# RWKV time mixing on one core: a weight's load between the halves of unit 0, coefficients worked out on rows, and one unit's transposes one step later

## The chip, the cores and the metric

The kernel runs on one core of a Trainium2 chip. The metric is device time in microseconds (us) of one execution. Five engines work beside each other, each in its own order: PE (matmul; its weight loads are shown apart as PEld), DVE (vector), ACT (scalar), POOL (GpSimd) and SP (which here only issues DMAs). They wait for each other through semaphores. ACT, POOL and SP issue DMAs; a queue's descriptors are worked off by 16 DMA engines.

## The reference

For x of 16 batches, 2048 tokens and 256 channels:

```python
x_prev[:, 1:, :] = x[:, :-1, :]
xv = x * time_mix_v + x_prev * (1 - time_mix_v)
xr = x * time_mix_r + x_prev * (1 - time_mix_r)
v = xv.reshape(-1, d_model) @ value_weight
r = xr.reshape(-1, d_model) @ receptance_weight
r_sigmoid = 1.0 / (1.0 + np.exp(-r))
out = (r_sigmoid * v).reshape(-1, d_model) @ output_weight
```

The key path (xk, k) does not enter the output, and the kernel does not compute it.

## The kernel before, in words

A **unit** is 512 tokens, so there are 64 units, four to a batch. PE needs the channels on the partitions, so x is transposed first: for the first ten batches on PE (`transposes`, L260, into `ps_t`, copied to the transposed tiles `xt_...` by ACT), for the last ones by DMA. In the transposed tile the previous token is the same data one slot to the left, so no second copy of x is made.

Mixing is folded into the weights. With s = time_mix and p = 1 - s, x·s + x_prev·p = s·(x + c·x_prev) with c = 1/s - 1. The weights are scaled by s once (`w_bf`), and per unit DVE (with POOL and ACT helping) scales the previous tokens by c (`scale`, L351) and adds the tokens (`add`, L374) into `mix`. Only R of unit 0 is made without a mix (`project_unmixed`, L398): four matmuls for each half of the output channels, two with `w_prev` (the weight times p) on the previous tokens and two with `w_bf`.

For each unit, in the order in which the loop over g (L646) writes it, PE does R (`psum_r`, L384), transposes of a later unit (`advance`, L659), V (`psum_v`, L384) and the output product O of the unit before (`psum_o`, L416). ACT applies the sigmoid (L658), copies transposes (L289) and outputs (L471). DVE multiplies the sigmoid with V (`z_sb`, L697). The order on each engine is that of the program; nothing is rescheduled. `psum_r`, `psum_v` and `psum_o` have one buffer each, `ps_t` has two.

How far the transposes run ahead is set by the table `START_T` (L73): behind R of unit g they go up to unit `START_T[g]`, and the loads that `LOADS` (L79) ties to a unit are issued on POOL when `advance` gets to it. With unit 5, batch 1's second unit, goes the load of batch 3 (`(1, 1): (3,)`).

**The head.** SP loads units 0 and 1 of x as float32 in halves of two of their four 128-token columns (`load_halves`, half 1 ahead of half 0, into a tile of the `o_sb` pool), with the first weight (receptance) behind unit 0 and the value weight behind unit 1. ACT loads the four rows of time_mix_r and time_mix_v (`tm_rows`). POOL waits until the first weight has landed, and then issues casting loads (float32 to bfloat16): units 2 and 3, the output weight, batch 1 by units, and later whole batches. PE warms up on constants (`warm_up`, L201), transposes half 1, the four rows (L236), half 0 in two parts (L300), and goes on to R of unit 0, the transposes of unit 1, the second half of R, V of unit 0. `coefficients` (L234) copies the transposed rows from PSUM and makes s, p and c on 128 partitions by 4 columns.

Of the kernel before, what the change touches and what calls it, by code (L numbers as in the profile page):

```python
# [8 lines left out]
FP32 = mybir.dt.float32  # L9
BF16 = mybir.dt.bfloat16  # L10
ALU = mybir.AluOpType
# [4 lines left out]
def kernel(  # L16
# [25 lines left out]
    nc = tc.nc  # L42

    B, S, D = x.shape
    P = 128
    KO = D // P
# [8 lines left out]
    H = UJ // 2  # L55
# [14 lines left out]
    PAD = 16  # L70
    SPARE = 9 * UB // 2
    NX, NO = 4, 7
    START_T = [1, 3, 5, 6, 7, 9, 11, 12]  # L73
    AHEAD = 6
    PAIRS = 10
    WARM = 25
# [14 lines left out]
    consts = ctx.enter_context(tc.tile_pool(name="consts", bufs=1))  # L91
# [20 lines left out]
    loads = {}  # L112
# [7 lines left out]
    ident_f = consts.tile([P, P], FP32)  # L120
# [26 lines left out]
    def load(b):  # L147
        if b < STAGED:
            x_bf[b] = xpool.tile([P, J, D], BF16, name="x_bf")
        if b < BYUNIT:  # L150
            for e in range(UB):
                nc.gpsimd.dma_start(  # L152
                    out=x_bf[b][:, e * UJ : (e + 1) * UJ, :], in_=unit_rows(x, b, e)[:, 0]
                )
            return
        if b in HALVED:
            return [
                nc.gpsimd.dma_start(out=x_bf[b][:, j : j + J // 2], in_=rows(b)[:, j : j + J // 2])
                for j in (0, J // 2)
            ]  # L160
        run = 8192 if b < LONG else 16384
        return nc.gpsimd.dma_start(out=x_bf[b], in_=rows(b), max_dma_last_dim=run)  # L162

    x_unit = opool.tile([P, 2, UJ, D], FP32, name="o_sb")
    tm_rows = consts.tile([2 * KO, P], FP32)
    w_f32 = consts.tile([P, 2, KO, D], FP32)
    for m, tm in enumerate([time_mix_r, time_mix_v]):
        nc.scalar.dma_start(
            out=tm_rows[m * KO : (m + 1) * KO, :], in_=tm.rearrange("(ko p) -> ko p", p=P)
        )  # L170

    def load_halves(e):
        for h in (1, 0):
            nc.sync.dma_start(  # L174
                out=x_unit[:, e, h * H : (h + 1) * H],
                in_=unit_rows(x, 0, e)[:, 0, h * H : (h + 1) * H, :],
            )

    load_halves(0)
    first_weight = nc.sync.dma_start(  # L180
        out=w_f32[:, 0], in_=receptance_weight.rearrange("(ko p) n -> p ko n", p=P)
    )
    load_halves(1)
    nc.sync.dma_start(out=w_f32[:, 1], in_=value_weight.rearrange("(ko p) n -> p ko n", p=P))
    sig0 = consts.tile([P, 1], BF16)
    nc.scalar.activation(out=sig0, in_=zeros[:, 0:1], func=ACT.Sigmoid)
# [1 line left out]
    w_prev = consts.tile([P, KO, D], BF16)  # L188
    wo_bf = consts.tile([P, KO, D], BF16)
    x_first = xpool.tile([P, 2, UJ, D], BF16, name="x_bf")  # L190
    for e in (2, 3):
        op = nc.gpsimd.dma_start(out=x_first[:, e - 2], in_=unit_rows(x, 0, e)[:, 0])  # L192
        if e == 2:
            tc.add_manual_dep(op.ins, first_weight.ins.name, SYNC, reason="behind the weight")
    nc.gpsimd.dma_start(out=wo_bf, in_=output_weight.rearrange("(ko p) n -> p ko n", p=P))  # L195
    load(1)

    ones = nc.const_aps.tensor_like(1.0, zeros)
    wide = nc.const_aps.tensor_like(1.0, wo_bf.rearrange("p k d -> p (k d)"))
# [10 lines left out]
    def new_xt(b):  # L210
        if b >= BYUNIT:
            for group in GROUPS:
                if b != group[0]:
                    continue
                if b >= STAGED:
                    t = xtpool.tile([P, KO, len(group) * (PAD + S)], BF16, name="xt_both")
                    for k in range(len(group)):
                        xt[b + k] = t[:, :, k * (PAD + S) + PAD - 1 : (k + 1) * (PAD + S)]
                    xt_both[b] = t
                    return  # L220
                xt_both[b] = xtpool.tile([P, J + 1, KO, len(group), P], BF16, name="xt_both")
                for k in range(len(group)):
                    xt[b + k] = xt_both[b][:, :, :, k]
                    nc.gpsimd.memset(xt[b + k][:, 0, :, 0:1], 0.0)
            return
        xt[b] = consts.tile([P, UB * (UJ + 1), KO, P], BF16, name=f"xt_first{b}")
        (nc.vector if b == 0 else nc.gpsimd).memset(xt[b][:, 0, :, 0:1], 0.0)

    new_xt(0)
    tms = consts.tile([P, 2, KO], FP32)  # L230
    c_sb = consts.tile([P, 2, KO], FP32)
    tm_prev = consts.tile([P, 2, KO], FP32)

    def coefficients():  # L234
        ps = ps_o_pool.tile([P, 2, KO], FP32, name="psum_o")
        nc.tensor.transpose(  # L236
            out=ps.rearrange("p m k -> p (m k)"), in_=tm_rows, identity=ident_f[: 2 * KO, : 2 * KO]
        )
        tm = consts.tile([P, 2, KO], FP32)
        nc.vector.tensor_copy(out=tm, in_=ps)  # L240
        nc.vector.tensor_scalar(
            out=tms, in0=tm, scalar1=0.0, scalar2=1e-30, op0=ALU.is_equal, op1=ALU.mult
        )
        nc.vector.tensor_tensor(out=tms, in0=tms, in1=tm, op=ALU.add)
        nc.vector.tensor_scalar(
            out=tm_prev, in0=tm, scalar1=-1.0, scalar2=1.0, op0=ALU.mult, op1=ALU.add
        )
        nc.vector.reciprocal(c_sb, tms)
        nc.vector.tensor_scalar(out=c_sb, in0=c_sb, scalar1=-1.0, scalar2=None, op0=ALU.add)

    def by_dma(b, after):

# [42 lines left out]
    def first_transposes():  # L295
        def part(lo, n, pool, name):
            ps = pool.tile([P, n, KO, P], FP32, name=name)
            for jj in range(n):
                for ko in range(KO):
                    nc.tensor.transpose(  # L300
                        out=ps[:, jj, ko],
                        in_=x_unit[:, 0, lo + jj, ko * P : (ko + 1) * P],
                        identity=ident_f,
                    )
            nc.scalar.copy(out=xt[0][:, 1 + lo : 1 + lo + n], in_=ps)
            return ps

        ps = part(H, H, ps_r_pool, "psum_r")
        nc.scalar.copy(out=xt[0][:, 0, :, 1:P], in_=ps[:, H - 1, :, 0 : P - 1])
        coefficients()  # L310
        part(0, 1, ps_v_pool, "psum_v")
        part(1, 1, ps_o_pool, "psum_o")

    def slots(piece, off=0):

        b, _, lo, hi = piece
        j = lo // P + (lo // TU if b < BYUNIT else 0) + off
        return slice(j, j + (hi - lo) // P)
# [32 lines left out]
    def scale(piece, kos=(0, 1)):  # L351
        b, m, _, _ = piece
        for ko in kos:
            nc.vector.tensor_scalar(  # L354
                out=mixed(piece, ko),
                in0=tokens(piece, 0, ko),
                scalar1=c_sb[:, m, ko : ko + 1],
                scalar2=None,
                op0=ALU.mult,
            )  # L360
# [205 lines left out]
    def advance(limit):  # L566
        nonlocal tnext
        while tnext <= min(limit, NU - 1):
# [4 lines left out]
                transposes(tnext)  # L573
            tnext += 1

    first_transposes()
    for ko in range(KO):
        nc.vector.tensor_scalar(
            out=w_prev[:, ko, :],
            in0=w_f32[:, 0, ko, :],  # L580
            scalar1=tm_prev[:, 0, ko : ko + 1],
            scalar2=None,
            op0=ALU.mult,
        )
    nc.vector.tensor_scalar(
        out=w_bf[:, 0, 0, :], in0=w_f32[:, 0, 0, :], scalar1=tms[:, 0, 0:1], scalar2=None, op0=ALU.mult
    )
    nc.scalar.activation(
        out=w_bf[:, 0, 1, :], in_=w_f32[:, 0, 1, :], func=ACT.Copy, scale=tms[:, 0, 1:2]
    )  # L590
    scale(pieces(0)[1])
    add(pieces(0)[1])
    for ko in range(KO):
        nc.vector.tensor_scalar(
            out=w_bf[:, 1, ko, :],
            in0=w_f32[:, 1, ko, :],
            scalar1=tms[:, 1, ko : ko + 1],
            scalar2=None,
            op0=ALU.mult,
# [11 lines left out]
    first = {}  # L611
# [34 lines left out]
    for g in range(NU - 1):  # L646
# [48 lines left out]
        n = TU // 2 if g == NU - 2 else TU  # L695
        for c in range(0, TU, n):
            nc.vector.tensor_tensor(  # L697
                out=z_sb[:, :, c : c + n],
                in0=s_sb[:, :, c : c + n],
                in1=ps_v[:, :, c : c + n],  # L700
                op=ALU.mult,
# [47 lines left out]
```

## Time and profile before

| | us |
|---|---|
| median of three runs | 199.56 |
| lowest and highest run | 198.65, 200.79 |
| span of the profiled execution | 197.1 |
| PE busy in it | 191.5 |
| DVE, ACT, POOL busy | 183.1, 177.1, 86.3 |

For the profiled execution the page gives its span, from the first instruction to the last, and no other time; what lies around the span is in the runs' times alone. Rows of a timeline read: start, busy time, engine, line, operation, output and inputs, count, and in brackets the idle time before it and who ended it. Rows of the chain read: start, length, what. Rows of waits read: who waits, for whom, total, times, longest. Rows of DMA issues read: tile, queue, count, KB, time from issue to landing.

### The profile page before, as it was taken

How to read it: one execution, taken by the hardware profiler on the slowest of the kernel's cores; microseconds unless marked ns; L12 is line 12 of the kernel's file. 1: busy time of each engine (PE TensorE's matmuls, PEld its weight loads, DVE VectorE, ACT ScalarE, POOL GpSimd, SP SyncE). 2: the span in 40 equal slices, each digit the busy share in tenths (PEclk: the TensorE clock that was granted, in tenths of full speed). 3: DMA queues.
4: the chain of work that ended last, by engine and by line, in shares of the span. 5: the costliest groups of instructions: out<-in, count | busy, mean ns of one | idle time of the engine just before them, and what ended most of it. 6: DMA issues, size and time to landing. Idle time of an engine off the chain costs nothing.

```text
span 197.1 us, 3735 instructions
## 1 busy us (share of the span) xinstructions
PE 191.5 (97%) x1358; PEld 123.0 (62%) x1364; DVE 183.1 (93%) x286; ACT 177.1 (90%) x197; POOL 86.3 (44%) x117
## 2 busy tenths in 40 slices
PE   8999999999999999999999999999999999999992
PEld 3556676666666666666666666666666666666660
DVE  0999999999999999999999999999999999999962
ACT  3699899999999999999999999999999999999982
POOL 2845542443665635624334266444433444444200
PEclk9999999999999999999999999999999999999998
DMA  5999999999999999999999999999999999999985
GB/s 185 238 176 224 218 254 262 247 259 262 296 413 283 283 296 332 283 238 198 376 209 290 335 346 186 212 218 241 290 290 419 419 421 419 416 416 421 382 327 221
DMA packets 35593, 58.13 MB, mean 295 GB/s; under 512 B 26004, under 2 KB 27128, under 8 KB 30840
## 3 DMA queue, kind: packets, MB, share of 16 engines
q1 hardware_dynamic: 31792, 41.34, 60.3%
q0 software_dynamic: 3632, 16.44, 41.6%
q8 instruction: 10, 0.16, 0.3%
q10 hardware_dynamic: 152, 0.13, 0.2%
q14 instruction: 7, 0.06, 0.1%
HBM read 34.34 MB, written 39.90 MB: 377 GB/s over the span
## 4 chain that ended last, share of the span: by engine, by line
PE 90%; DMA 6%; POOL 1%; issue 0%; SPq 0%; ACT 0%
PE psum_r L384 27%; PE psum_v L384 27%; PE psum_o L416 27%; PE ps_t L272 8%; DMA x_bf<-in_x_dram 4%; DMA w_f<-n_receptance_weight_dram 2%; PE ps_t L416 1%; POOL x_bf L192 1%; SPq L174 0%; POOL wo_bf L195 0%; PE psum_v L416 0%; POOL x_bf L152 0%; PE ps_t L384 0%; PE psum_r L416 0%; ACT x_bf L446 0%
## 5 line engine op out<-in xcount | busy, mean ns | idle before, releaser
L364 POOL TENSOR_SCALAR mix<-xt_both,c_sb 128x1024 bf16<-128x1024 bf16 (+1 forms) x55 | 61.1, 1110 | 85.5 <-DVE mix L376 82.3
L697 DVE TENSOR_TENSOR z_sb<-s_sb,psum_v 128x1024 bf16<-128x1024 bf16 (+1 forms) x64 | 76.8, 1201 | 2.3 <-PE psum_v L384 1.1
L376 DVE TENSOR_TENSOR mix<-mix,xt_both 128x1024 bf16<-128x1024 bf16 x112 | 76.8, 696 | 1.4
L384 PEld LDWEIGHTS <-w_bf 128*128 128x128 bf16 x512 | 48.5, 98 | 39.2 <-DVE mix L376 0.8
L658 ACT ACTIVATE s_sb<-psum_r 128x1024 bf16<-128x1024 f32 x63 | 65.2, 1034 | 6.2 <-PE psum_r L384 6.0
L384 PE MATMUL psum_v<-mix,w_bf 128*128 128x512 bf16 (+1 forms) x252 | 64.8, 378 | 0.4 <-DVE mix L376 0.2
L384 PE MATMUL psum_r<-mix,w_bf 128*128 128x512 bf16 x250 | 64.6, 379 | 0.2
L416 PE MATMUL psum_o<-wo_bf,z_sb 128*128 128x256 bf16 x486 | 63.2, 273 | 0.0
L416 PEld LDWEIGHTS <-z_sb 128*128 128x128 bf16 x512 | 52.0, 103 | 17.9 <-DVE z_sb L510 0.7
L471 ACT COPY o_sb<-psum_o 128x1024 f32<-128x1024 f32 x50 | 51.2, 1023 | 5.0 <-PE psum_o L416 4.8
L289 ACT COPY xt_both<-ps_t 128x1024 bf16<-128x1024 bf16 x32 | 32.9, 1039 | 0.0
L272 PEld LDWEIGHTS <-x_bf 128*128 128x128 bf16 x304 | 19.8, 98 | 8.4 <-DMA x_bf<-in_x_dram 0.4
L272 PE MATMUL ps_t<-ident,x_bf 128*128 128x128 bf16 x304 | 22.7, 219 | 0.2 <-DMA x_bf<-in_x_dram 0.2
L354 DVE TENSOR_SCALAR mix<-xt_both,c_sb 128x1024 bf16<-128x1024 bf16 (+1 forms) x47 | 21.3, 463 | 0.0
L638 ACT ACTIVATE mix<-xt_both,c_sb 128x1024 bf16<-128x1024 bf16 x14 | 16.3, 1163 | 0.0
L376 DVE TENSOR_TENSOR mix<-mix,xt_first 128x1024 bf16<-128x1024 bf16 x15 | 10.5, 708 | 0.1
L471 ACT COPY x_bf<-psum_o 128x1024 f32<-128x1024 f32 x10 | 10.2, 1015 | 0.0
L354 DVE TENSOR_SCALAR mix<-xt_first,c_sb 128x512 bf16<-128x512 bf16 x22 | 6.6, 350 | 0.3 <-ACT xt_first L282 0.2
L289 ACT COPY xt_first<-ps_t 128x1024 bf16<-128x1024 bf16 x6 | 6.0, 1022 | 0.0
L557 POOL COPY xt_first<-xt_first 128x254 bf16<-128x254 bf16 x5 | 2.0, 392 | 7.2 <-DVE mix L376 7.2
L162 POOL DMA_DIRECT2D x_bf<-in_x_dram x8 | 4.7, 584 | 0.0
L364 POOL TENSOR_SCALAR mix<-xt_first,c_sb 128x512 bf16<-128x512 bf16 x6 | 4.1, 685 | 1.3 <-DVE mix L376 0.8
(68 smaller groups left out, 52.3 us busy)
## 6 DMA issues: line engine op xcount, KB each, us to landing
out_dram<-o_sb SPq DMA_DIRECT2D x25, 1024.0 KB, 12.1
x_bf<-in_x_dram POOLq DMA_DIRECT2D x8, 1024.0 KB, 15.8
x_natural<-in_x_dram POOLq DMA_DIRECT2D x4, 1024.0 KB, 11.8
out_dram<-x_bf SPq DMA_DIRECT2D x4, 1024.0 KB, 14.4
x_natural<-in_x_dram POOLq DMA_DIRECT2D x4, 512.0 KB, 12.7
out_dram<-x_bf SPq DMA_DIRECT2D x4, 512.0 KB, 4.7
x_bf<-in_x_dram POOLq DMA_DIRECT2D x6, 256.0 KB, 7.0
o_sb<-in_x_dram SPq DMA_DIRECT2D x4, 256.0 KB, 3.9
```

The costliest lines, as they stand in the source:

```text
L162: return nc.gpsimd.dma_start(out=x_bf[b], in_=rows(b), max_dma_last_dim=run)
L272: nc.tensor.transpose(out=ps[:, jj], in_=src[:, jj, ko * P : (ko + 1) * P], identity=idn)
L289: nc.scalar.copy(out=xt[b][:, j0 : j0 + UJ], in_=ps)
L354: nc.vector.tensor_scalar(out=mixed(piece, ko), in0=tokens(piece, 0, ko), scalar1=c_sb[:, m, ko : ko + 1], scalar2=None, op0=ALU.mult,)
L364: op = nc.gpsimd.tensor_scalar(out=mixed(piece, 1), in0=tokens(piece, 0, 1), scalar1=c_sb[:, m, 1:2], scalar2=1.0, op0=ALU.mult, op1=ALU.mult,
L376: return nc.vector.tensor_tensor(out=mixed(piece), in0=mixed(piece), in1=tokens(piece, 1), op=ALU.add)
L384: nc.tensor.matmul(out=ps[:, mo, :], lhsT=w_bf[:, m, ko, mo * P : (mo + 1) * P], rhs=mixed((b, m, e * TU + lo, e * TU + hi), ko), start=(k ...
L416: nc.tensor.matmul(out=ps[:, j, :], lhsT=slot[:, ko, j], rhs=wo_bf[:, ko, :], start=(ko == 0), stop=(ko == KO - 1),)
L471: nc.scalar.copy(out=o[:, j0 : j0 + UJ, :], in_=ps)
L638: nc.scalar.activation(out=mixed(piece, ko), in_=tokens(piece, 0, ko), func=ACT.Copy, scale=c_sb[:, m, ko : ko + 1],)
L658: nc.scalar.activation(out=s_sb, in_=ps_r, func=ACT.Sigmoid)
L697: nc.vector.tensor_tensor(out=z_sb[:, :, c : c + n], in0=s_sb[:, :, c : c + n], in1=ps_v[:, :, c : c + n], op=ALU.mult,)
```

## The change

Five things are done.

1. On SP's queue the first weight stands between the two halves of unit 0 instead of behind them.
2. s and p are made on the four rows of time_mix (4 partitions by 128 columns, tiles `coef_rows`) before PE transposes them; PE transposes two tiles instead of one, and DVE makes one copy of both results.
3. c's last step, the subtraction of 1, stands behind the scaling of the first weight.
4. The casting loads on POOL wait for that copy on DVE instead of for the first weight's landing. They are written behind `first_transposes`.
5. `START_T[2]` is 4 instead of 5: the transposes of unit 5, and with them the load of batch 3, come behind R of unit 3.

```diff
-    START_T = [1, 3, 5, 6, 7, 9, 11, 12]
+    START_T = [1, 3, 4, 6, 7, 9, 11, 12]
...
+    coef_rows = [consts.tile([2 * KO, P], FP32, name=f"coef_rows{n}") for n in range(2)]
...
-    load_halves(0)
-    first_weight = nc.sync.dma_start(
+    load_half(0, 1)
+    nc.sync.dma_start(
         out=w_f32[:, 0], in_=receptance_weight.rearrange("(ko p) n -> p ko n", p=P)
     )
-    load_halves(1)
+    load_half(0, 0)
+    load_half(1, 1)
+    load_half(1, 0)
...
-    for e in (2, 3):
-        op = nc.gpsimd.dma_start(out=x_first[:, e - 2], in_=unit_rows(x, 0, e)[:, 0])
-        if e == 2:
-            tc.add_manual_dep(op.ins, first_weight.ins.name, SYNC, reason="behind the weight")
-    nc.gpsimd.dma_start(out=wo_bf, in_=output_weight.rearrange("(ko p) n -> p ko n", p=P))
-    load(1)
+    def cast_loads(after):
+        for e in (2, 3):
+            op = nc.gpsimd.dma_start(out=x_first[:, e - 2], in_=unit_rows(x, 0, e)[:, 0])
+            if e == 2:
+                tc.add_manual_dep(op.ins, after.ins.name, SYNC, reason="behind the first loads")
+        nc.gpsimd.dma_start(out=wo_bf, in_=output_weight.rearrange("(ko p) n -> p ko n", p=P))
+        load(1)
...
+    coefs = consts.tile([P, 2, 2, KO], FP32)
+    tms, tm_prev = (coefs[:, n] for n in range(2))
     c_sb = consts.tile([P, 2, KO], FP32)
+    row_s, row_prev = coef_rows
+    nc.vector.tensor_scalar(
+        out=row_s, in0=tm_rows, scalar1=0.0, scalar2=1e-30, op0=ALU.is_equal, op1=ALU.mult
+    )
+    nc.vector.tensor_tensor(out=row_s, in0=row_s, in1=tm_rows, op=ALU.add)
+    nc.vector.tensor_scalar(
+        out=row_prev, in0=tm_rows, scalar1=-1.0, scalar2=1.0, op0=ALU.mult, op1=ALU.add
+    )
 
     def coefficients():
+        ps = ps_o_pool.tile([P, 2, 2, KO], FP32, name="psum_o")
+        for n, row in enumerate(coef_rows):
+            nc.tensor.transpose(
+                out=ps[:, n].rearrange("p m k -> p (m k)"),
+                in_=row,
+                identity=ident_f[: 2 * KO, : 2 * KO],
+            )
+        op = nc.vector.tensor_copy(out=coefs, in_=ps)
         nc.vector.reciprocal(c_sb, tms)
-        nc.vector.tensor_scalar(out=c_sb, in0=c_sb, scalar1=-1.0, scalar2=None, op0=ALU.add)
+        return op
...
-    first_transposes()
+    cast_loads(first_transposes())
...
+    nc.vector.tensor_scalar(out=c_sb, in0=c_sb, scalar1=-1.0, scalar2=None, op0=ALU.add)
     scale(pieces(0)[1])
```

Where the instructions stand now. First SP's queue at the start of the program, before (`o_sb` is where the halves of units 0 and 1 go, `w_f_100` holds both weights):

```order
L174 DMA o_sb<-in_x_dram 128x512 x2
L180 DMA w_f_100<-in_receptance_weight_dram 128x2x256
L174 DMA o_sb<-in_x_dram 128x512 x2
L184 DMA w_f_100<-in_value_weight_dram 128x2x256
L474 DMA out_dram<-o_sb 128x2x1024 x4
```

and of the changed kernel:

```order
L174 DMA o_sb<-in_x_dram 128x512
L180 DMA w_f_102<-in_receptance_weight_dram 128x2x256
L174 DMA o_sb<-in_x_dram 128x512 x3
L186 DMA w_f_102<-in_value_weight_dram 128x2x256
L482 DMA out_dram<-o_sb 128x2x1024 x4
```

The weight moved one place up and half 0 of unit 0 one place down. Next DVE at the start of the program, before (`tm` is the copy of the transposed rows, `tms` is s, `tm_prev` is p, `c_sb` is c):

```order
L240 COPY tm<-psum_o 128x4
L241 TENSOR_SCALAR tms<-tm 128x4
L244 TENSOR_TENSOR tms<-tms,tm 128x4
L245 TENSOR_SCALAR tm_prev<-tm 128x4
L248 RECIPROCAL c_sb<-tms 128x4
L249 TENSOR_SCALAR c_sb<-c_sb 128x4
L578 TENSOR_SCALAR w_prev<-w_f_100,tm_prev 128x256 x2
L585 TENSOR_SCALAR w_bf<-w_f_100,tms 128x256
L354 TENSOR_SCALAR mix<-xt_first_131,c_sb 128x4x128 x2
```

and of the changed kernel (`coefs` holds s and p):

```order
L238 TENSOR_SCALAR coef_rows_100<-tm_rows 4x128
L241 TENSOR_TENSOR coef_rows_100<-coef_rows_100,tm_rows 4x128
L242 TENSOR_SCALAR coef_rows_101<-tm_rows 4x128
L254 COPY coefs<-psum_o 128x8
L255 RECIPROCAL c_sb<-coefs 128x4
L586 TENSOR_SCALAR w_prev<-w_f_102,coefs 128x256 x2
L593 TENSOR_SCALAR w_bf<-w_f_102,coefs 128x256
L599 TENSOR_SCALAR c_sb<-c_sb 128x4
L362 TENSOR_SCALAR mix<-xt_first_125,c_sb 128x4x128 x2
```

Three small steps moved ahead of the copy from PSUM and one behind the weights. Last ACT around units 2 and 3, before, from the sigmoid of unit 2 on (`xt_first_311` is the transposed tile of batch 1, so its copies are those of units 4 and up):

```order
L658 ACTIVATE s_sb<-psum_r 128x1024
L289 COPY xt_first_311<-ps_t 128x1024 x2
L471 COPY o_sb<-psum_o 128x1024
L658 ACTIVATE s_sb<-psum_r 128x1024
L289 COPY xt_first_311<-ps_t 128x1024
L471 COPY o_sb<-psum_o 128x1024
```

and of the changed kernel:

```order
L667 ACTIVATE s_sb<-psum_r 128x1024
L296 COPY xt_first_312<-ps_t 128x1024
L479 COPY o_sb<-psum_o 128x1024
L667 ACTIVATE s_sb<-psum_r 128x1024
L296 COPY xt_first_312<-ps_t 128x1024 x2
L479 COPY o_sb<-psum_o 128x1024
```

The copy of unit 5's transposes moved past the output copy of unit 1 and the sigmoid of unit 3. On PE the eight transposes of unit 5 moved likewise, past V of unit 2, O of unit 1 and R of unit 3.

More of the change, by code (lines that the diff above doesn't have):

```diff
@@ L170, with load_half @@
         )
[L172 to L177, printed above, removed]
-    load_halves(0)
-    first_weight = nc.sync.dma_start(
+    def load_half(e, h):
+        nc.sync.dma_start(
+            out=x_unit[:, e, h * H : (h + 1) * H],
+            in_=unit_rows(x, 0, e)[:, 0, h * H : (h + 1) * H, :],
+        )
+    load_half(0, 1)
+    nc.sync.dma_start(
         out=w_f32[:, 0], in_=receptance_weight.rearrange("(ko p) n -> p ko n", p=P)
     )
-    load_halves(1)
+    load_half(0, 0)
+    load_half(1, 1)
+    load_half(1, 0)
     nc.sync.dma_start(out=w_f32[:, 1], in_=value_weight.rearrange("(ko p) n -> p ko n", p=P))
@@ L229 @@
     new_xt(0)
-    tms = consts.tile([P, 2, KO], FP32)
+    coefs = consts.tile([P, 2, 2, KO], FP32)
+    tms, tm_prev = (coefs[:, n] for n in range(2))
     c_sb = consts.tile([P, 2, KO], FP32)
-    tm_prev = consts.tile([P, 2, KO], FP32)
-    def coefficients():
[L235 to L247, printed above, removed]
+    row_s, row_prev = coef_rows
[6 more added lines that the diff above has]
+    )
+    def coefficients():
+        ps = ps_o_pool.tile([P, 2, 2, KO], FP32, name="psum_o")
[4 more added lines that the diff above has]
+                identity=ident_f[: 2 * KO, : 2 * KO],
+            )
+        op = nc.vector.tensor_copy(out=coefs, in_=ps)
         nc.vector.reciprocal(c_sb, tms)
-        nc.vector.tensor_scalar(out=c_sb, in0=c_sb, scalar1=-1.0, scalar2=None, op0=ALU.add)
+        return op
     def by_dma(b, after):
@@ L309, in first_transposes @@
         nc.scalar.copy(out=xt[0][:, 0, :, 1:P], in_=ps[:, H - 1, :, 0 : P - 1])
-        coefficients()
+        after = coefficients()
         part(0, 1, ps_v_pool, "psum_v")
         part(1, 1, ps_o_pool, "psum_o")
+        return after
     def slots(piece, off=0):
```

## The prediction

> **What bounds the kernel now.** I name the work of a unit u (512 tokens): Ru and Vu are its two projections on PE, Tu the transposes of its x, Ou its output product, zu the product on DVE (L697). First the page: its span and the busy times.
>
> ```profile
> span 197.1 us, 3735 instructions
> PE 191.5 (97%) x1358; PEld 123.0 (62%) x1364; DVE 183.1 (93%) x286; ACT 177.1 (90%) x197; POOL 86.3 (44%) x117
> ```
>
> PE is busy 97%. The change leaves PE's work as it is but for one 4-row transpose, so only 197.1 - 191.5 = 5.6 us of PE idling can be won at all. The table of waits, PE alone, says where it waits for others:
>
> ```profile
> PE psum_r L398 <- ACT xt_first L305: 0.3, 1, 0.3
> PE psum_v L384 <- DVE mix L376: 0.2, 1, 0.2
> PE ps_t L272 <- DMA x_bf<-in_x_dram: 0.2, 1, 0.2
> ```
>
> That is 0.7 us, all of it before 16 us (the rows below). So the question is when PE's stream gets going, and whether anything stops it later. The chain in order of time shows what the change is aimed at:
>
> ```profile
> 1.20 0.41 SPq L174
> ...
> 1.66 3.62 DMA w_f<-n_receptance_weight_dram
> 5.28 0.30 issue
> 5.58 0.74 POOL x_bf L192
> ...
> 8.12 7.37 DMA x_bf<-in_x_dram
> ```
>
> Behind half 1 of unit 0, SP issues half 0 at 1.20 and the first weight at 1.66. The weight lands at 5.28, POOL waits for that before it issues the casting loads (5.58), and the load of unit 5's x, issued at 8.12, lands at 15.49. Then the stream on PE and the engines that feed it:
>
> ```profile
> 0.78 2.83 PE L204 MATMUL ps_t<-const-bfloat16-1.0 128*128 128x512 bf16 x7 [0.78 <-PEq L733]
> ...
> 4.57 0.23 PE L236 MATMUL psum_o<-ident_f,tm_rows 4*128 4x4 f32 x1
> 4.73 0.44 PE L300 MATMUL psum_v<-ident_f,o_sb 128*128 128x128 f32 x2
> 5.05 0.44 PE L300 MATMUL psum_o<-ident_f,o_sb 128*128 128x128 f32 x2
> ...
> 6.14 0.73 PE L398 MATMUL psum_r<-xt_first,w_prev 128*128 128x512 bf16 x2 [0.26 <-ACT xt_first L305]
> ...
> 7.17 1.04 PE L272 MATMUL ps_t<-ident_f,o_sb 128*128 128x128 f32 x8
> 8.05 0.59 PE L398 MATMUL psum_r<-xt_first,w_prev 128*128 128x512 bf16 x2
> ...
> 8.91 1.03 PE L384 MATMUL psum_v<-mix,w_bf 128*128 128x512 bf16 x4
> ...
> 14.72 0.61 PE L272 MATMUL ps_t<-ident,x_bf 128*128 128x128 bf16 x8
> 15.54 0.62 PE L272 MATMUL ps_t<-ident,x_bf 128*128 128x128 bf16 x8 [0.21 <-DMA x_bf<-in_x_dram]
> 16.00 1.03 PE L384 MATMUL psum_v<-mix,w_bf 128*128 128x512 bf16 x4
> ...
> 19.04 1.03 PE L384 MATMUL psum_v<-mix,w_bf 128*128 128x512 bf16 x4
> ...
> 31.85 0.61 PE L272 MATMUL ps_t<-ident,x_bf 128*128 128x128 bf16 x8
> ```
>
> Matmuls overlap, so I read paces from start to start: a free half of R0 takes 8.91 - 8.05 = 0.86, a group of eight bf16 transposes 16.00 - 15.54 = 0.46, and V2 to V3, a whole unit, 3.04. The first half of R0 took 7.17 - 6.14 = 1.03: it was held up by 0.17.
>
> **Part 1, the weight between the halves.** What the halves' landing costs shows in the DMA issues of 1.2 to 1.3 us and in ACT's timeline:
>
> ```profile
> o_sb<-in_x_dram SPq DMA_DIRECT2D x1, 256.0 KB, 3.4
> ```
> ```profile
> 5.42 0.39 ACT L305 CAST xt_first<-psum_v 128x256 bf16<-128x256 f32 x1
> 5.68 0.41 ACT L305 CAST xt_first<-psum_o 128x256 bf16<-128x256 f32 x1
> ...
> 7.81 1.07 ACT L282 CAST xt_first<-ps_t 128x512 bf16<-128x512 f32 x2 [1.32 <-PE ps_t L272]
> ...
> 20.98 1.01 ACT L471 COPY o_sb<-psum_o 128x1024 f32<-128x1024 f32 x1 [0.20 <-PE psum_o L416]
> ```
>
> Half 0 landed at 1.20 + 3.4 = 4.6, and its transposes started at 4.73, 0.13 behind. Half and weight have 256 KB each (the page's issues), on one queue. With their places exchanged, I take it that their landings are exchanged too: weight 4.6, half 0 5.28. Then half 0's transposes start at 5.4; they end 5.49 - 4.73 = 0.76 later, at 6.16; ACT, which was 0.19 behind them before (5.49 to 5.68), is free by then and copies until 6.6; R0 starts 0.05 behind (as 6.09 to 6.14), at 6.65. Undisturbed it takes 0.86 and T1 starts at 7.5 instead of 7.17: **+0.35 us**. Ends: if half 0 still landed at 4.6, R0 would start at 6.14 as now and run free, -0.17; if a half that follows a weight lands 0.2 later than that weight did, +0.55. I stay near the exchange, since the landings are those of three equal transfers in a queue.
>
> **Part 2, coefficients on rows.** DVE before, from its timeline:
>
> ```profile
> 4.83 0.16 DVE L240 COPY tm<-psum_o 128x4 f32<-128x4 f32 x1 [3.96 <-PE psum_o L236]
> ...
> 5.72 0.69 DVE L578 TENSOR_SCALAR w_prev<-w_f,tm_prev 128x256 bf16<-128x256 f32 x2
> 6.34 0.33 DVE L585 TENSOR_SCALAR w_bf<-w_f,tms 128x256 bf16<-128x256 f32 x1
> 6.60 0.65 DVE L354 TENSOR_SCALAR mix<-xt_first,c_sb 128x512 bf16<-128x512 bf16 x2
> ...
> 8.91 0.67 DVE L354 TENSOR_SCALAR mix<-xt_first,c_sb 128x512 bf16<-128x512 bf16 x2 [0.17 <-ACT xt_first L282]
> ...
> 14.82 0.80 DVE L376 TENSOR_TENSOR mix<-mix,xt_first 128x1024 bf16<-128x1024 bf16 x1
> ...
> 17.13 1.22 DVE L697 TENSOR_TENSOR z_sb<-s_sb,psum_v 128x1024 bf16<-128x1024 bf16 x1
> ...
> 20.26 1.22 DVE L697 TENSOR_TENSOR z_sb<-s_sb,psum_v 128x1024 bf16<-128x1024 bf16 x1
> ```
>
> Copy to w_prev is 5.72 - 4.83 = 0.89 for six small steps. Three of them move ahead, into the 3.96 that DVE sits idle; one (the -1) moves behind w_bf. Left are copy and reciprocal, about 0.4 (each 0.16 long as the copy, and a little between), behind one more transpose of 0.16 (4.57 to 4.73): copy at 5.0, w_prev at 5.4 (the weight is there by Part 1) until 6.05, w_bf until 6.35, the -1 until 6.5. All of it is done when half 0 lets R0 start at 6.65. So this saves 0.3 on DVE and **0** at the end; what hid its predecessor is now half 0. It takes away the 0.17 that held R0, which is counted above. Were the rows of time_mix to land only at 4.57 (by then they had, for PE transposed them), the three steps, 0.5 by the 0.16 of the copy, would put w_bf at 6.85, where R0's third matmul wants it 0.43 after its start, 7.08: still 0.
>
> V0's scaling waits for the same copies: 6.65 against 6.60. Unit 1's scaling waits for ACT's copies of T1, which end 0.35 later, 9.23 against 8.88; from there DVE is 0.3 to 0.35 late, and V2 waits for DVE (next part).
>
> **Part 3, casting loads behind the copy of the coefficients.** POOL's wait ends at 5.15 (end of the copy) instead of 5.28. If POOL again needs 0.30, the loads go out at 5.45, 0.13 earlier; if it needs 0.05, 0.4 earlier. Who waits for them? T5 alone (0.21), and that is settled below: **0**. The cost is that they share the engines with the value weight's load for so much longer; at half each, that load is at most 0.2 late, at 7.9 to 8.0, and DVE wants it at 7.9: 0 to 0.1. The Trainium skill (DMA: Bandwidth & Descriptors, Queues, rings and completion order) has each engine take turns between the queues it has work for, packet by packet: by that rule this sharing is real and the upper end, +0.1, would be right. No row here shows the two queues side by side at a changed start.
>
> **Part 4, T5 behind R3.** In unit 2, T4 starts at 14.72 and T5 at 15.54, 0.21 of it waiting. Without T5, PE is done with T4 at 15.18, but V2 needs DVE's add, 14.82 + 0.80 = 15.62. So V2 starts at 15.66, not 15.18: 0.34 won of the 0.82 left free. What is late next is DVE. T5's 0.46 now stands between R3 and V3: 15.66 + 3.04 + 0.46 = 19.16 against 19.04. So this edit by itself is +0.12 at V3, and z3 could follow 1.13 behind V3 (as 16.00 to 17.13) at 20.29. It started at 20.26 before, with no idle time of DVE ahead of it (the row has none), so DVE set it and the late V3 costs 0.03. I take **0**, with ends -0.1 and +0.1. With Part 1's shift both bounds move alike: V2 at 16.0, V3 at 19.5. ACT gets T5's copy, 0.9, in unit 3; it had 0.20 idle there (20.98), so O2's copy and the sigmoid behind it come up to 0.7 later, of which 0.3 is the shift that all have. Only z4 waits for that sigmoid: 0 to 0.4, and I take 0, since DVE too is late by then.
>
> With T5 its load(3) moves too, on POOL from 15.08 past unit 3's scaling to about 18.7, right ahead of load(4). POOL's timeline, and these two issues in the windows at 15.2 and 18.5 us:
>
> ```profile
> 15.08 0.58 POOL L162 DMA_DIRECT2D x_bf<-in_x_dram  x1
> ...
> 18.29 0.58 POOL L162 DMA_DIRECT2D x_bf<-in_x_dram  x1
> ```
> ```profile
> x_bf<-in_x_dram POOLq DMA_DIRECT2D x1, 1024.0 KB, 14.9
> ```
> ```profile
> x_bf<-in_x_dram POOLq DMA_DIRECT2D x1, 1024.0 KB, 17.9
> ```
>
> They landed at 30.0 and 36.2, 6.2 apart although issued 3.2 apart: the queue sets that, and load(3) starts moving some 6 before it lands, at about 24. Handed in at 18.7 it still lands near 30, ahead of T12 at 31.85: 0.
>
> **Sum.** +0.35 + 0 + 0 + 0, with 0.05 of rounding in favour of absorbed waits: **+0.3 us**; ends -0.3 and +1.1. The span would be 197.4. The median of the runs is 199.56, 2.46 above the profiled span (the page has no other time for that execution), and I leave that difference alone: 199.9.
>
> **Rivals.**
> *Half 0 is not late* (0.17). If the engines finish the half about as early as now, R0 runs freed of its 0.17 hold: -0.2, with the ends of Part 4 -0.1 to -0.3: 199.3. For it: the three transfers are in flight together. Against: half 0 and weight landed in their order, 0.7 apart.
> *The array stays slow* (0.06), the slower side. Its place is the new hole on PE, 4.9 to 5.4, in the warm-up. The six and a quarter warm-up matmuls took 2.83, 0.45 each for 512 columns, against 0.22 (0.86 / 4) from 8.05 on, so PE ran at half pace from 0.78 until 3.6 at least and 8.05 at most. If the hole makes it begin again at 5.4 and that lasts 4, between those 2.8 and 7.3, PE does half of what it could until 9.4: 2.0 lost, with +0.3 together 201.9. It decides if the transposes of T1 start to start take over 1.5 instead of 0.88. Against: the hole is 0.5, a seventh of that time. The Trainium skill (TensorE: Matmul & The Clock Gate, Part 1) has the clock fall back only after an idle window of about 3.4 us; by that this rival falls.
> *load(3) comes late* (0.03): if its 14.9 counted from the issue, it would land at 18.7 + 14.9 = 33.6 and T12 would wait 1.75: 201.6. Against it stand the even landings.
> *Forecast* (0.70), 199.6 to 200.7. The rest (0.04) is what I don't see.
>
> **Numbers.** Runs of one kernel spread from 198.65 to 200.79 here, so a median may be off by some 0.7 either way. The first two cases with that give 198.6 to 201.1; I take 198.5 to 201.2, which leaves out the two slow rivals. About 1% (2.0 us) is what can be told from no change: 197.56 and 201.56. Both likely cases lie well inside; faster 0.04, same 0.89, slower 0.07.
>
> **What would show it.** After: half 0's transposes on PE at 5.3 to 5.5 with a wait for DMA before them; w_prev on DVE at about 5.4; R0 at 6.65, its two halves free; T1 at 7.5; no wait for DMA at T5; V2 near 16.0 behind DVE, V3 near 19.5; T12 without a wait. I am wrong if half 0's transposes start before 5.0, if V3 starts before 19.0, or if PE waits over 0.3 anywhere behind 20 us.

## The result, and the profile after

| | us |
|---|---|
| changed kernel, median of 22 runs (lowest, highest) | 201.38 (199.59, 203.25) |
| kernel before, median of 22 runs beside them (lowest, highest) | 199.23 (198.65, 201.21) |
| ratio, with its 95% interval | 1.0086 (1.0066 to 1.0106) |
| profiled execution of the changed kernel: time, span | 199.59, 197.8 |

The ratio says 1.7 us slower (0.0086 x 199.23), with the interval 1.3 to 2.1. The medians are 2.15 apart and the means, without the one disturbed execution of 203.25, 1.64 (201.09 and 199.45): the changed kernel's runs crowd between 201.2 and 201.7, and its median lies in that crowd. The forecast was +0.3. The profile alone would mislead here: the execution that it shows, 199.59, is the shortest of the 22, and 13 of them took 201.22 to 201.72. So the profile is read first as what it is, a lucky execution; what the others do differently is shown by the experiments.

The page of the changed kernel, span and busy times:

```profile
span 197.8 us, 3737 instructions
PE 191.5 (97%) x1359; PEld 123.0 (62%) x1365; DVE 183.6 (93%) x286; ACT 177.1 (90%) x197; POOL 86.2 (44%) x117
```

PE's work is what it was, so the 0.7 of longer span is idling. The waits of PE, those of the head:

```profile
PE psum_v L307 <- DMA o_sb<-in_x_dram: 0.8, 1, 0.8
PE psum_v L392 <- DVE mix L384: 0.4, 1, 0.4
```

The wait of T5 for DMA is gone, and one for half 0 has come. PE's timeline (start, busy time, and in brackets the idle time ahead):

```profile
0.78 2.83 PE L208 MATMUL ps_t<-const-bfloat16-1.0 128*128 128x512 bf16 x7 [0.78 <-PEq L742]
3.50 1.04 PE L307 MATMUL psum_r<-ident_f,o_sb 128*128 128x128 f32 x4
4.47 0.28 PE L249 MATMUL psum_o<-ident_f,coef_rows 4*128 4x4 f32 x2
5.52 0.44 PE L307 MATMUL psum_v<-ident_f,o_sb 128*128 128x128 f32 x2 [0.76 <-DMA o_sb<-in_x_dram]
...
6.69 0.59 PE L406 MATMUL psum_r<-xt_first,w_prev 128*128 128x512 bf16 x2
7.12 0.59 PE L406 MATMUL psum_r<-xt_first,w_bf 128*128 128x512 bf16 x2
7.55 1.04 PE L279 MATMUL ps_t<-ident_f,o_sb 128*128 128x128 f32 x8
8.42 0.59 PE L406 MATMUL psum_r<-xt_first,w_prev 128*128 128x512 bf16 x2
...
16.00 1.04 PE L392 MATMUL psum_v<-mix,w_bf 128*128 128x512 bf16 x4 [0.36 <-DVE mix L384]
...
19.51 1.03 PE L392 MATMUL psum_v<-mix,w_bf 128*128 128x512 bf16 x4
```

Half 0's transposes stand 0.79 later than before (5.52 for 4.73), R0 0.55 later but free of the old hold-up (its first half takes 0.86 from start to start), T1 0.38 and V3 0.47 later. The hole that the change makes in PE's warm-up is 0.76, at 4.76 to 5.52.

DVE's timeline, and the issue of the first casting load (the last number is the time from issue to landing):

```profile
5.09 0.58 DVE L586 TENSOR_SCALAR w_prev<-w_f,coefs 128x256 bf16<-128x256 f32 x2
```
```profile
x_bf<-in_x_dram POOLq DMA_DIRECT2D x1, 256.0 KB, 5.1
```

The first weight is scaled at 5.09 instead of 5.72: DVE is early, as worked out. The casting load is a surprise: before, the same load landed after

```profile
x_bf<-in_x_dram POOLq DMA_DIRECT2D x1, 256.0 KB, 3.8
```

Now it is in flight for 1.3 longer.

### The profile page after: what moved, and what is told of

Same layout as the page of the kernel before. It is cut to its first block, busy times and chain, and to the rows that moved or that the text cites. A ratio compares the mean times of both kernels' runs of the same rounds, so it can differ in the third digit from the quotient of the medians.

```text
span 197.8 us, 3737 instructions
## 1 busy us (share of the span) xinstructions
PE 191.5 (97%) x1359; PEld 123.0 (62%) x1365; DVE 183.6 (93%) x286; ACT 177.1 (90%) x197; POOL 86.2 (44%) x117
## 4 chain that ended last, share of the span: by engine, by line
PE 91%; DVE 3%; DMA 2%; ACT 1%; issue 1%; POOL 0%; SPq 0%; DVEq 0%; POOLq 0%
PE psum_v L392 27%; PE psum_r L392 27%; PE psum_o L424 26%; PE ps_t L279 8%; DMA o_sb<-in_x_dram 2%; PE ps_t L424 1%; DVE mix L384 1%; DVE mix L362 1%; DVE z_sb L706 1%; ACT xt_first L289 1%; PE psum_r L406 1%; POOL mix L372 0%; ACT xt_first L312 0%; PE psum_v L424 0%; PE psum_v L307 0%
```

## Experiments

Each kernel but the repeats changes one or a few things of one of the two kernels; all compute the whole result, and the warm-up matmuls that some add work on constants and are used by nothing. Each ran 12 times. The kernel before had medians of 199.30 beside e1 to e4, 199.12 beside e5 to e8 and 199.35 beside e9 to e12; differences below are to these.

**e1: the changed kernel again**, for another execution to look at. No edit.

> The changed kernel again, unchanged, for a second profile and more times. Its 22 runs have a median of 201.38 against 199.23 before, 2.15 more, while the one profiled execution (199.59) is the shortest of all and its span is only 0.7 longer than the span profiled before. Theory A (slow array): in most executions the array is still at half pace when R of unit 0 begins, since PE idles for 0.76 us before half 0; a profile of a typical run has a span of 199.4 to 199.9 and shows 512-column matmuls 0.43 us apart, not 0.22, for some time behind 5.5 us, and nothing else late. Theory B (late loads): a typical profile shows PE waiting for casting loads, 1 us or more, between 9 and 35 us, at full pace.

Median 201.14, +1.84; ratio 1.0049 (1.001 to 1.0088). Its profiled execution took 201.39, about the median, with a span of 199.6. PE's timeline in it:

```profile
3.62 1.09 PE L307 MATMUL psum_r<-ident_f,o_sb 128*128 128x128 f32 x4
4.64 0.37 PE L249 MATMUL psum_o<-ident_f,coef_rows 4*128 4x4 f32 x2
5.72 0.69 PE L307 MATMUL psum_v<-ident_f,o_sb 128*128 128x128 f32 x2 [0.71 <-DMA o_sb<-in_x_dram]
...
7.38 1.06 PE L406 MATMUL psum_r<-xt_first,w_prev 128*128 128x512 bf16 x2
8.23 1.06 PE L406 MATMUL psum_r<-xt_first,w_bf 128*128 128x512 bf16 x2
9.09 1.31 PE L279 MATMUL ps_t<-ident_f,o_sb 128*128 128x128 f32 x8
10.23 0.59 PE L406 MATMUL psum_r<-xt_first,w_prev 128*128 128x512 bf16 x2
```

Here is the missing time, as theory A has it. Two matmuls of R0 follow each other in 0.85 (7.38 to 8.23), where the other execution took 0.43 (6.69 to 7.12): the array runs at half pace behind the hole, through the first half of R0 and part of T1 (9.09 to 10.23 is 1.14, for 0.87). The second half of R0 starts at 10.23 instead of 8.42, 1.81 later, and the span is 1.8 longer. Nothing behind that adds to it. The granted clock in the page's PEclk row reads 9 (90% or more) in every slice of both executions, and the mean by core is 1.00, so the pace is to be had from starts alone.

**e4: only the load order**, on the kernel before.

```diff
...
-    load_halves(0)
+    load_half(0, 1)
     first_weight = nc.sync.dma_start(
...
-    load_halves(1)
+    load_half(0, 0)
+    load_half(1, 1)
+    load_half(1, 0)
```

> The kernel before with only the load order changed (first weight between unit 0's halves); coefficients, casting loads behind the weight and the transposes of unit 5 as before. Theory A: PE idles from about 4.8 to 5.5 as in the changed kernel, so the median is 1.5 to 2.2 above before: ratio 1.007 to 1.011. Theory B: casting loads go out at the weight's landing, 0.7 earlier than before; a ratio of 1.000 to 1.003.

Median 201.09, +1.8; ratio 1.0044 (1.0007 to 1.008). The 12 runs fall in two groups: four at 199.07 to 199.25, where the kernel before is, and eight at 200.86 to 202.47. The profiled one, 201.0, is of the second:

```profile
6.14 0.69 PE L301 MATMUL psum_v<-ident_f,o_sb 128*128 128x128 f32 x2 [1.24 <-DMA o_sb<-in_x_dram]
...
7.80 1.06 PE L399 MATMUL psum_r<-xt_first,w_prev 128*128 128x512 bf16 x2
8.65 0.91 PE L399 MATMUL psum_r<-xt_first,w_bf 128*128 128x512 bf16 x2
9.40 1.04 PE L273 MATMUL ps_t<-ident_f,o_sb 128*128 128x128 f32 x8
```

The load order alone brings the half pace (0.85 from 7.80 to 8.65). How much of the loss it brings depends on what is compared: by the medians 1.8 of 2.15, as theory A expected, by the ratios 0.9 of 1.7, between the two theories.

**e2 and e12: the changed kernel with the load order undone**, run on two occasions.

```diff
+    load_half(0, 0)
     nc.sync.dma_start(
         out=w_f32[:, 0], in_=receptance_weight.rearrange("(ko p) n -> p ko n", p=P)
     )
-    load_half(0, 0)
     load_half(1, 1)
```

> The changed kernel with only the load order undone (half 0 ahead of the first weight, as before). Theory A: half 0 lands at about 4.5, PE's hole of 0.76 closes, and the median falls to that of the kernel before or up to 0.3 below it: ratio 0.998 to 1.001. Theory B: casting loads stay where they are in the changed kernel, so the ratio stays at about 1.007 to 1.010.

> The changed kernel with only the load order undone, once more, in one call with the kernel without the move of unit 5's transposes. If the 0.95 of the first time was there by right: ratio 1.003 to 1.008 again, and by the difference to its neighbour the move of unit 5's transposes costs 0.1 to 0.3 beside the other parts; if it was chance, 1.001 to 1.003.

Medians 200.25 and 200.19, +0.95 and +0.84; ratios 1.0056 (1.003 to 1.0082) and 1.0039 (1.0009 to 1.007). That is neither what theory A expected (1.001 at most) nor theory B (1.007 at least): something is left without the hole. Neither profiled execution has a hole ahead of half 0, but they do not switch to full pace at the same point. PE's timeline of e2, and then of e12:

```profile
3.64 0.63 PE L307 MATMUL psum_r<-ident_f,o_sb 128*128 128x128 f32 x4
4.20 0.28 PE L249 MATMUL psum_o<-ident_f,coef_rows 4*128 4x4 f32 x2
...
6.46 0.65 PE L406 MATMUL psum_r<-xt_first,w_prev 128*128 128x512 bf16 x2 [0.89 <-DVE w_prev L586]
```
```profile
4.91 0.69 PE L307 MATMUL psum_v<-ident_f,o_sb 128*128 128x128 f32 x2
5.39 0.64 PE L307 MATMUL psum_o<-ident_f,o_sb 128*128 128x128 f32 x2
5.82 0.69 PE L208 MATMUL ps_t<-const-bfloat16-1.0 128*128 128x512 bf16 x4
6.49 0.59 PE L406 MATMUL psum_r<-xt_first,w_prev 128*128 128x512 bf16 x2
```

In e2 already the first four transposes are fast (0.63, where e1 takes 1.09); in e12 the two of `psum_v` are still slow (0.69, for 0.44), the warm-up at 5.82 takes 0.69 for the 0.55 of other executions, so it ran slow for 0.28, until about 6.1, and R0 at 6.49 is fast. Without a hole the switch thus comes between 3.64 and about 6.1, which is 2.9 to 5.3 behind PE's first matmul at 0.77.

What is left is seen in part. In e2, PE waits 0.89 for `w_prev` ahead of R0, since the first weight took 4.2 to land, for 3.6 before; T1 is 0.45 late with that (7.62 for 7.17). In e12 it took 3.6, and PE doesn't wait there. Both executions (199.95 and 199.35) lie below the medians of their kernels, so what the slower ones do is open.

**e6: only the casting loads moved**, on the kernel before.

```diff
...
-    for e in (2, 3):
-        op = nc.gpsimd.dma_start(out=x_first[:, e - 2], in_=unit_rows(x, 0, e)[:, 0])
-        if e == 2:
-            tc.add_manual_dep(op.ins, first_weight.ins.name, SYNC, reason="behind the weight")
...
+    def cast_loads(after):
...
-        nc.vector.tensor_copy(out=tm, in_=ps)
+        op = nc.vector.tensor_copy(out=tm, in_=ps)
...
-    first_transposes()
+    cast_loads(first_transposes())
```

> The kernel before with the casting loads behind DVE's copy of the coefficients instead of behind the first weight's landing; nothing else. Theory B: the casting loads start some 0.2 earlier, share the DMA engines with the last halves and the value weight, and land these or unit 2 later: ratio 1.002 to 1.006. Theory A: PE's stream keeps its gaps, ratio 0.999 to 1.001.

Median 199.07, ratio 1.0009 (0.9986 to 1.0033): no difference, as theory A expected. But the profiled execution, 200.78, was one of the three of 12 above 200.2, and in it half 0 came late by itself, with the loads in their old order:

```profile
5.97 0.69 PE L303 MATMUL psum_v<-ident_f,o_sb 128*128 128x128 f32 x2 [1.13 <-DMA o_sb<-in_x_dram]
...
7.62 1.06 PE L402 MATMUL psum_r<-xt_first,w_prev 128*128 128x512 bf16 x2
8.48 0.90 PE L402 MATMUL psum_r<-xt_first,w_bf 128*128 128x512 bf16 x2
```

A hole of 1.13, and half pace behind it (0.86 for two). The half pace goes with the hole, then, not with the order of the queue.

**e9 and e10: the hole by itself, and the hole filled.** To part the hole from every load, e9 leaves all loads of the kernel before alone and lets the first transpose of half 0 wait for DVE's last coefficient; e10 puts two warm-up matmuls of 512 columns into that hole.

```diff
...
-        def part(lo, n, pool, name):
+        def part(lo, n, pool, name, after=None):
...
+                    if after is not None and jj + ko == 0:
+                        tc.add_manual_dep(op.ins, after.ins.name, SYNC, reason="a hole")
...
-        coefficients()
-        part(0, 1, ps_v_pool, "psum_v")
+        after = coefficients()
+        warm_up(FILL)
+        part(0, 1, ps_v_pool, "psum_v", after)
```

`coefficients` returns the instruction that makes p; the line `warm_up(FILL)`, with `FILL = 8`, is in e10 alone.

> The kernel before, all loads and instructions as they were, but half 0's first transpose also waits for DVE's p (the step that ended at 5.47 in the profile before), so that PE idles from about 4.8 to 5.5 as in the changed kernel. Theory A: by the wait itself R of unit 0 is 0.3 to 0.7 late; on top of that most executions stay at half pace until 9 to 9.5 us and lose 1.2 to 1.8 more: the median is 1.5 to 2.2 above before, with a few executions near 199.5. Theory B (loads): only the wait itself counts, 0.3 to 0.7, and no execution shows 512-column matmuls 0.43 apart behind 5.5 us.

> The same wait, with two 512-column warm-up matmuls on PE in the hole (0.43 us at full pace, 0.86 at half). The transposes start when they did in the kernel with the hole, or up to 0.1 later. Theory A: the median falls by 0.8 to 1.5 against the kernel with the hole. Theory B: no difference, within 0.3.

With the hole: median 200.36, +1.0 where theory A expected 1.5 to 2.2, seven of 12 runs at 200.19 to 202.49 and five at 199.15 to 199.59; ratio 1.0028 (0.9996 to 1.0059). With the hole filled: median 199.48, all 12 within 199.28 to 199.67; ratio 0.9991 (0.997 to 1.0012). The intervals overlap, so the difference between the two lies in the groups of runs, not in the ratios. PE's timeline of e9 and of e10:

```profile
3.67 1.09 PE L301 MATMUL psum_r<-ident_f,o_sb 128*128 128x128 f32 x4
4.69 0.26 PE L236 MATMUL psum_o<-ident_f,tm_rows 4*128 4x4 f32 x1
5.69 0.44 PE L301 MATMUL psum_v<-ident_f,o_sb 128*128 128x128 f32 x2 [0.74 <-DVE tm_prev L245]
...
6.87 0.59 PE L401 MATMUL psum_r<-xt_first,w_prev 128*128 128x512 bf16 x2
```
```profile
4.96 0.61 PE L205 MATMUL ps_t<-const-bfloat16-1.0 128*128 128x512 bf16 x2
5.76 0.44 PE L302 MATMUL psum_v<-ident_f,o_sb 128*128 128x128 f32 x2 [0.20 <-DVE tm_prev L246]
...
6.94 0.59 PE L403 MATMUL psum_r<-xt_first,w_prev 128*128 128x512 bf16 x2
```

The half 0 transposes and R0 start at the same time in both, 0.07 apart. All that differs is how long PE idles ahead of them, 0.74 or 0.20, and without the longer idling the upper group of runs disappears. In e10's profiled execution the array was at full pace when the filling began (0.61 for its two matmuls), so what the filling does is read from the 12 times and not from these rows. e9's profiled execution, 199.59, is of the lower group (the transposes behind the hole take 0.44); that the upper one runs at half pace behind the hole is inferred from e1, e4 and e6, not seen.

**e3 and e5: the hole of the load filled**, in the changed kernel (e3) and in e4's (e5).

```diff
+    FILL = 12
...
+        warm_up(FILL)
         part(0, 1, ps_v_pool, "psum_v")
```

> The changed kernel with twelve more warm-up columns of 128 (three matmuls of 512 on constants, 0.65 us at full pace, 1.35 at half) on PE between the coefficients' transposes and half 0's, so that PE does not idle while it waits for half 0; no load moves. Theory A: the hole is filled, the array is at full pace by R of unit 0 in nearly all runs, and the median is 0.3 to 0.7 above the kernel before: ratio 1.001 to 1.004. Theory B: nothing changes, ratio 1.007 to 1.010; if the fill only delays half 0's transposes, more than that.

> The kernel before with the load order changed and three 512-column warm-up matmuls put in the hole ahead of half 0. Against the load order alone (median 201.09, 1.8 above before). Theory A (the hole keeps the array at half pace): the loss goes back to the 0.3 of the later R of unit 0, ratio 1.000 to 1.003. Theory B (late loads of unit 2, which made PE wait 1.33 us in the filled kernel's profile): the fill changes nothing, ratio 1.005 to 1.010, and T2 waits for its load.

e3: median 201.33, ratio 1.0099 (1.0062 to 1.0136), no gain at all; theory A expected 1.004 at most. e5: 199.86, +0.74, ratio 1.0035 (1.001 to 1.0059), between the two theories. By the medians it wins back 1.1 of e4's 1.8, and two of its 12 runs lie above 200.8, where eight of e4's did; by the ratios (1.0044 and 1.0035) a gain is not shown. Their PE timelines, e3's first:

```profile
4.57 0.83 PE L209 MATMUL ps_t<-const-bfloat16-1.0 128*128 128x512 bf16 x3
...
6.69 0.59 PE L408 MATMUL psum_r<-xt_first,w_prev 128*128 128x512 bf16 x2
...
11.64 0.62 PE L280 MATMUL ps_t<-ident,x_bf 128*128 128x128 bf16 x8 [1.33 <-DMA x_bf<-in_x_dram]
```
```profile
4.69 1.43 PE L206 MATMUL ps_t<-const-bfloat16-1.0 128*128 128x512 bf16 x3
6.01 0.44 PE L302 MATMUL psum_v<-ident_f,o_sb 128*128 128x128 f32 x2
...
7.19 0.59 PE L401 MATMUL psum_r<-xt_first,w_prev 128*128 128x512 bf16 x2
...
11.77 0.62 PE L274 MATMUL ps_t<-ident,x_bf 128*128 128x128 bf16 x8 [0.95 <-DMA x_bf<-in_x_dram]
```

R0 is at full pace in both. In e5 the filling itself ran at half pace (1.32 for three matmuls, 4.69 to 6.01) and the transposes behind it at full pace (0.44), so the array switched at about 6.0; in e4, with the hole, it was still slow at 8.65. In e3 it was at full pace already when the filling began (0.83 for three). But then T2 waits for unit 2's casting load, 1.33 and 0.95. DMA issues of that load, in e3 and in e5:

```profile
x_bf<-in_x_dram POOLq DMA_DIRECT2D x1, 256.0 KB, 6.4
```
```profile
x_bf<-in_x_dram POOLq DMA_DIRECT2D x1, 256.0 KB, 6.2
```

In e1 that load took 5.6 and nobody waited, since T2 starts at 11.96 there: the half pace hid it. So the costs of hole and load do not add up. Six of e3's 12 runs, at 201.7 to 203.1, lie above its profiled one (200.65); what happens in those no profile shows, and it stays open.

**e7: only the rows and the moved -1**, on the kernel before.

```diff
-    START_T = [1, 3, 4, 6, 7, 9, 11, 12]
+    START_T = [1, 3, 5, 6, 7, 9, 11, 12]
...
-    nc.sync.dma_start(
+    load_half(0, 0)
+    first_weight = nc.sync.dma_start(
...
-    load_half(0, 0)
...
+    cast_loads(first_weight)
...
-    cast_loads(first_transposes())
+    first_transposes()
```

This is written against the changed kernel, with the other edits taken back.

> The kernel before with only the coefficients worked out on rows and the -1 of c behind the weight's scaling. By the sum of the prediction DVE is 0.3 us earlier at the first weight, which then sets R of unit 0 by its landing: ratio 0.998 to 1.000. If DVE's order costs something (the loss left in the kernel with the load order undone, 0.95, would be here), 1.002 to 1.005.

Median 199.45, +0.33; ratio 1.0016 (0.9994 to 1.0038). The PE timeline:

```profile
6.23 0.65 PE L408 MATMUL psum_r<-xt_first,w_prev 128*128 128x512 bf16 x2 [0.34 <-DVE w_prev L588]
```

R0 starts at 6.23, for 6.14, and waits for `w_prev`, where before it waited for ACT's copy. DVE has the coefficients early and waits 0.60 for the first weight, which took 4.1 to land here (3.6 before): without the new load order there is nothing for the earlier coefficients to gain.

**e8: only T5 moved**, on the kernel before.

```diff
-    START_T = [1, 3, 5, 6, 7, 9, 11, 12]
+    START_T = [1, 3, 4, 6, 7, 9, 11, 12]
```

> The kernel before with only the transposes of unit 5 moved behind R of unit 3. By the prediction's sum: V2 earlier by up to 0.34, V3 later by 0.1, nothing behind it: ratio 0.9995 to 1.001. If the second group of transposes in unit 3 delays ACT and is not made up for later: +0.4 to +0.9, ratio 1.002 to 1.0045.

Median 199.29, +0.17; ratio 1.0011 (0.9986 to 1.0036). The PE timeline:

```profile
15.58 1.04 PE L384 MATMUL psum_v<-mix,w_bf 128*128 128x512 bf16 x4 [0.33 <-DVE mix L376]
...
19.08 1.03 PE L384 MATMUL psum_v<-mix,w_bf 128*128 128x512 bf16 x4
```

V2 starts 0.42 earlier, behind DVE, and V3 0.04 later: what is won ahead of V2 is given back ahead of V3.

**e11: rows and casting loads, without load order and T5.**

```diff
-    START_T = [1, 3, 4, 6, 7, 9, 11, 12]
+    START_T = [1, 3, 5, 6, 7, 9, 11, 12]
...
+    load_half(0, 0)
     nc.sync.dma_start(
...
-    load_half(0, 0)
```

> The changed kernel with the load order and the transposes of unit 5 as before: what is left is the coefficients on rows and the casting loads behind their copy, which then comes some 0.5 earlier than the first weight's landing. Alone the parts measured 1.0016 and 1.0009. If they add up, 1.002 to 1.003; if the early casting loads together with rows make the loss of 0.95 of the kernel with only the load order undone, 1.004 to 1.006.

Median 199.83, +0.48; ratio 1.0018 (0.9987 to 1.005). The PE timeline:

```profile
5.96 0.64 PE L406 MATMUL psum_r<-xt_first,w_prev 128*128 128x512 bf16 x2
...
10.69 0.62 PE L279 MATMUL ps_t<-ident,x_bf 128*128 128x128 bf16 x8 [1.01 <-DMA x_bf<-in_x_dram]
```

R0 is 0.18 earlier than in the kernel before, the best start of all, and it is lost to a wait of 1.01 for unit 2, whose load took 5.3 here. Beside e12 on the same occasion (+0.84), T5's move on top of this costs about 0.36, where it cost 0.17 alone; both intervals overlap, so its size with the others is not settled.

## Why the prediction was right or wrong

**Part 1, the weight between the halves: right where it was costed, and short of the cost that mattered.** Half 0's transposes at 5.52 (said: 5.3 to 5.5, with a wait for DMA), R0 at 6.69 (6.65) with its halves free, T1 at 7.55 (7.5). In the profiled execution the +0.35 of a shifted stream is there.

**Part 2, rows: right.** `w_prev` at 5.09, earlier than the 5.4 said, and it bought nothing; e7 alone is within what a median can be off.

**Part 3, casting loads: mis-sized.** I asked what their sharing costs the value weight and took 0 to 0.1. What it costs is the other side, the loads themselves: unit 2 lands 5.1 behind its issue instead of 3.8, and 4.0 to 6.4 in the other kernels in which these loads start behind the copy. The 14 profiled executions fall apart by one thing, whether unit 0's halves and the first weight had all landed when POOL began with the casting loads. Where they had (before, e7 to e10, and e12), unit 2's load took 3.7 to 4.0; where the last of the three was still in flight (the other eight), it took 4.5 to 6.4. The wait for the weight in its old place, which the change gave up, kept the two apart. T2 waits 0.95 to 1.33 for that load in e3, e5 and e11. I had said that T5 alone waits for these loads; T2's load was left out of the sum, and it is the one that the sharing hits. The Trainium skill (DMA: Bandwidth & Descriptors, Queues, rings and completion order) has an engine take turns between the queues that it has work for; these rows agree that sharing costs, but no row here shows which engine gave the turns to whom. e6, which moves these loads alone, shows no loss in its median, so the later landing does not always cost time at the end. How much longer the load takes does not go by how long the transfers overlap: in e11 the weight landed about 0.15 behind POOL's start and the load took 5.3, in e2 it landed 0.9 behind and the load took 4.5. That stays open.

**Part 4, T5 behind R3: right.** V2 at 16.00 behind DVE (16.0), V3 at 19.51 (19.5), no wait at T5 or T12; e8 shows the exchange by itself.

**The sum, +0.3, is that of the profiled execution** (V3 0.47 late, and the span 0.7 longer; the V products start 0.38 later at 100 us and 0.68 later at 185, and where the 0.3 between arises I have not traced). It is not that of the median.

**The step that failed is the chance of a rival.** "The array stays slow" was given 0.06 and 201.9. By the times it is what happens in most executions, and the rows show it in e1: at 201.39 that is this rival, its span 2.5 above the one of before where 2.3 was worked out. Two arguments had put it aside. One was that the hole is a seventh of the slow time; but whether PE falls back to half pace is not the question while it has not yet left it. In e1, e4 and e6 the hole comes before the switch, for the four transposes ahead of it still take 1.09; the switch is then put off: by the rows it comes at about 9.6 in e1, 9.3 in e4 and 9.1 in e6, 3.1 to 3.9 behind the hole's end (in e1, T1's 0.87 of work took 1.14, so it ran slow for 0.54; in e4 and e6, R0's second pair took 0.75 and 0.73 for 0.43, slow for 0.64 and 0.60). The other argument was a sentence of the Trainium skill (TensorE: Matmul & The Clock Gate, Part 1) on the fall back to the slow clock after an idle window of about 3.4 us. The same part of the Trainium skill states the one that bore on this: the first release needs a busy window, and the windows run on by themselves, in no fixed relation to the kernel's start. That agrees with the switch at 2.9 to 5.3 behind the first matmul, different from run to run, with the two groups of runs in e4 and e9, and with e10; the windows themselves no run here shows. Its 3.4 us is not borne out as a least time: the earliest switch here was 2.9 behind the first matmul, at the latest.

The rows of before could have dated the switch better than the prediction's 3.6 to 8.05. Half 1's four transposes take 1.02 from start to start at half pace (e1, 3.62 to 4.64) and 0.56 at full pace (e2, 3.64 to 4.20). Before they took 0.91 (3.66 to 4.57), and in the profile of the changed kernel 0.97 (3.50 to 4.47), so by this estimate both switched at about 4.4, less than 0.4 ahead of the hole at 4.76. A switch that comes a little later in another execution meets the hole.

Where the switch falls before the hole, as in the profiled execution of the changed kernel, or in it, as in e9's (the transposes ahead of the hole 1.02 from start to start, those behind it at full pace), the hole costs no more than itself. By their times, 4 of 12 runs in e4 and 5 of 12 in e9 were of this kind. The share of lucky executions is what I would have had to forecast, and one trace of before shows one switch only.

The point from which I let that rival decide was badly placed too: T1 over 1.5 from start to start. In e1 it is 1.14 and in e4 0.87, because by then the array is nearly or wholly at full pace again. R0's first half shows it: 0.85 for each pair.

**The range** ended at 201.2, below the median of 201.38, since it left out just this rival. Taken by the ratio, the changed kernel is at 200.9 (199.23 x 1.0086), inside the range; that is luck, for the +1.7 does not come from the terms that were added up to +0.3. The base of the forecast, 199.56, was a median of three runs and 0.33 above the median of 22.

## What to carry to other kernels

A hole in the warm-up of PE, even one of 0.7 us, can cost more than its length: 1.8 between the two profiled executions of the changed kernel, and not in every execution (8 of 12 lie in the upper group in e4, 7 of 12 in e9). So a load that is moved to the front of a queue has to be weighed by what it puts later among PE's first instructions, and a hole that must be there can be filled with matmuls on constants (e10); where a late load stands behind it, the filling alone can win nothing (e3). And one profile shows one execution: hold its time against all runs first, and where it lies at their edge, profile the same kernel again before explaining anything.

## What the runs showed that was not expected

- The switch of the array to full pace shows in no clock record here (the granted clock is 1.00 in the profiled executions of e1 and of the changed kernel alike) but in the starts: 0.43 or 0.22 per matmul of 512 columns.
- The hole filled made the times steadier than the kernel before itself: 199.28 to 199.67 over 12 runs, where the kernel before, beside it, had 198.52 to 201.20. It is no faster (0.9991, 0.997 to 1.0012), and none of the kernels tried beats the kernel before.
- The same half of 256 KB in the same place of the same queue can land over 1 us late: in e6 PE waited 1.13 for half 0, where the profile of the kernel before shows no wait. Since the order of the queue is the same in both, that kernel may have this hole now and then too.
